# Moving sides of 256 columns in a split-precision decoder layer

## The chip, the cores and the metric

The kernel runs on one core of one Trainium2 chip. The metric is the device time of one execution in microseconds, as the median of the runs; lower is better.

## What is computed

One decoder layer for a single sequence of 256 tokens with 2048 channels, all in float32:

```python
h    = rms_norm(x, norm_gain)
proj = h @ w_in          # [256, 8192]: h_conv | B | C | z_conv | q | k | v | z_attn, 1024 each
y_conv = short_gated_conv(h_conv, B, C, conv_w)            # B * causal 3-tap conv of (C * h_conv)
y_conv = rms_norm(y_conv, conv_out_gain) * silu(z_conv)
q, k   = per-head rms_norm of q and k                      # 8 heads of 128
y_attn = moba_attention(q, k, v)                           # 256 tokens are one block: causal attention
y_attn = rms_norm(y_attn, attn_out_gain) * silu(z_attn)
x      = x + concat([y_conv, y_attn]) @ w_out              # [256, 2048] @ [2048, 2048]
```

## The kernel before

Products of float32 operands are made from split operands: each operand is written as a high part, rounded to the type that TensorE (PE) takes, and a low part, the rest. A product is then three matmuls, high by high, high by low and low by high. ScalarE (ACT) makes the high parts (`wh`, line 462) and VectorE (DVE) the low ones (`wl`, line 463) of every piece of weights, three pieces ahead of the products (`LEAD`). SyncE issues the loads of the pieces.

The products run in three stages, one unit of weights after the other, each unit in pieces:

- Stage A, six units: q, k and v with tokens on the partitions, in chunks of 512 columns. The stationary side is a slice of x (`xs`), 128 channels by 128 tokens, and the weights move, 512 columns at a time. `by_parts` (lines 96 to 101) issues the three matmuls, one line each (99, 100, 101). A unit has 16 slices of channels and two of tokens, so 96 matmuls.
- Stage B, 20 units: the convolution's inputs and the gates with channels on the partitions, in groups of 256 channels. The weights are stationary, 128 channels by 128 columns, and x moves. `by_chan` (lines 466 to 471) moves both parts of x at once: line 470 multiplies `wh` by high and low part side by side, 512 columns, into a whole bank of `acc`, and line 471 adds `wl` by the high part to the first 256 columns. The bank's two halves still have to be added: `added` (lines 333 to 337) copies one half with ACT (line 335) and adds the other with DVE (line 336), and a further DVE product follows (lines 343, 347, 360, 364). A unit has 64 matmuls.
- Stage Y, eight units: the output product. Slices of y (`yh`, `yl`) are stationary, and `w_out` moves, 512 columns at a time, again through `by_parts`. The last unit is treated apart: it keeps three sums in `aux` banks, one of 512 columns for the first 128 tokens and two of 256 for the others, so that little is left to do after the last product.

Attention (`scores`, `attend` and the transposes) uses short matmuls of 128 and 256 columns on PE between the pieces of A and B. Work of the other engines is put into numbered slots (`at`), one for each piece, and issued after that piece's products. `acc` has two buffers of two banks, `aux` four of one.

Of the kernel before, what the change touches and what calls it, by code (L numbers as in the profile page):

```python
# [10 lines left out]
F32 = mybir.dt.float32  # L11
FR = mybir.dt.float32r
BF16 = mybir.dt.bfloat16
AF = mybir.ActivationFunctionType
# [3 lines left out]
P = 128  # L18
# [4 lines left out]
DG = 1024  # L23
CW = 512
HD = 128
NH = DG // HD
# [5 lines left out]
MASKED = -3.0e38  # L32
# w_in's columns: h_conv, b_gate, c_gate, z_conv, q, k, v, z_attn, DG each. q, k and v are computed with tokens on the
# partitions, in chunks of CW columns; the others with channels on the partitions, in groups of GW columns
A_ORDER = [(name, c) for c in range(DG // CW) for name in "qkv"]
B_ORDER = [("a", g) for g in range(NG)] + [(name, g) for g in range(NG) for name in "hcbz"]
FIRST = {name: n * DG for n, name in enumerate("hbczqkva")}
# columns of the parameter array
G_IN, G_Q, G_K, G_C, G_A, C_W = 0, 16, 17, 18, 26, 34
# [9 lines left out]
def hybrid_layer(ctx: ExitStack, tc: tile.TileContext, xT, x, w_a, w_b, w_out, par, out):  # L49
# [12 lines left out]

# [1 line left out]
    prm = cst.tile([P, NPAR], F32, name="prm")  # L64
# [12 lines left out]
    make_identity(nc, ident)  # L77
    # causal mask of the three blocks that a head has: (q0, k0), (q1, k0), (q1, k1)
    msk = cst.tile([P, 3, P], F32, name="msk")
# [4 lines left out]

# [1 line left out]
    todo = {}  # L86
# [4 lines left out]
    def then(slot, f, g, *args):  # L91
        """f now, g with f's result in a later slot"""
        r = f(*args)
        at(slot, g, *args, r)

    def by_parts(acc, stationary, moving, first, last):
        """the product of two split operands, without that of their low parts"""
        (sh, sl), (mh, ml) = stationary, moving
        nc.tensor.matmul(acc, sh, mh, start=first, stop=False)  # L99
        nc.tensor.matmul(acc, sh, ml, start=False, stop=False)  # L100
        nc.tensor.matmul(acc, sl, mh, start=False, stop=last)  # L101

    def rsqrt(dst, ms):
        nc.gpsimd.tensor_tensor(dst, ms, neg_half[:, :ms.shape[-1]], op=OP.pow)  # L104

    # sums of squares over channels, by partition and token: of x, of the attention, of the convolution
    sums = {}

    def add_squares(key, src):
        """src [P, 2, SEQ]"""  # L110
        sq = tp.tile([P, CW], F32, name="sq", bufs=2)
        nc.scalar.activation(sq, src, AF.Square)
        if key not in sums:
            s = sums[key] = cst.tile([P, SEQ], F32, name="sums_" + key)
            nc.vector.tensor_add(s, sq[:, :SEQ], sq[:, SEQ:])
        else:
            for i in range(2):
                nc.vector.tensor_add(sums[key], sums[key], sq[:, i * SEQ:(i + 1) * SEQ])
# [7 lines left out]
    def partition_sums(hi, lo):  # L126
        """on every partition"""
        a = aux()
        nc.tensor.matmul(a[:, :SEQ], ones, hi, start=True, stop=False)
        nc.tensor.matmul(a[:, :SEQ], ones, lo, start=False, stop=True)  # L130
        return a

    def by_token(dst, a):
        """dst [token, NT] from rows a [any, NT * token]"""
        for t in range(NT):
            d = tp.tile([P, P], F32, name="diag", bufs=2)
            nc.vector.tensor_tensor_reduce(out=d, in0=a[:, t * P:(t + 1) * P], in1=ident, scale=1.0, scalar=0.0,
                                           op0=OP.mult, op1=OP.add, accum_out=dst[:, t:t + 1])

    def token_sums(slot, key, f):  # L140
        """f gets the sums over channels [token, NT]"""
        def summed(a):
            ms = tp.tile([P, NT], F32, name="ms_t", bufs=2)
            by_token(ms, a)
            f(ms)

        at(slot, lambda: at(slot + 2, lambda hl=split_rows(sums[key]): at(slot + 3, summed, partition_sums(*hl))))

# [1 line left out]
    xs = cst.tile([P, KT, 2, SEQ], FR, name="xs")  # L150
# [13 lines left out]

    # rx by token on the partitions; rxb, its square rx2b by token along the free axis
    rx = cst.tile([P, NT], F32, name="rx")
# [16 lines left out]

    # y, transposed and split for the products
    yh = cst.tile([P, KT, SEQ], FR, name="yh")
    yl = cst.tile([P, KT, SEQ], FR, name="yl")

# [1 line left out]
    qk_0, v_sb, sq, ssq_h, r_h, qn = {}, {}, {}, {}, {}, {}  # L189
# [65 lines left out]
    def mask(h):  # L255
        # s = -(scale * masked score); its minimum is -max
        s = pr[h] = tp.tile([P, 3 * P], F32, name="s", bufs=3)
        mx[h] = tp.tile([P, NT], F32, name="mx", bufs=2)
        m = msk.rearrange("p b k -> p (b k)")
        for t, sl in parts:  # L260
            nc.vector.tensor_tensor_reduce(out=s[:, sl], in0=sc[h][:, sl], in1=m[:, sl], scale=-scale, scalar=3.0e38,
                                           op0=OP.add, op1=OP.min, accum_out=mx[h][:, t:t + 1])
# [38 lines left out]

# [1 line left out]
    def split_y(y, kt, col):  # L303
# [13 lines left out]
    def c_rms(ms):  # L317
        # the convolution lacks a factor rx: r_c = rx * (rx ** 2 * mean square + EPS) ** -0.5
        nc.vector.tensor_mul(ms, ms, rx)
        nc.vector.tensor_mul(ms, ms, rx)  # L320
        nc.vector.tensor_scalar(ms, ms, 1.0 / DG, EPS, op0=OP.mult, op1=OP.add)
        rsqrt(r_c, ms)
# [3 lines left out]

# [1 line left out]
    h_sb, u_sb, cv, yc, z_sb = {}, {}, {}, {}, {}  # L328

    def by_channel(rows):  # L330
        return rows[:, None, :].to_broadcast([P, GPT, SEQ])

    def added(acc):
        d = t2k((P, GPT, SEQ))
        nc.scalar.activation(d, acc[:, :, SEQ:], AF.Copy)  # L335
        nc.vector.tensor_add(d, acc[:, :, :SEQ], d)  # L336
        return d

    def h_done(g, acc):
        h_sb[g] = added(acc)  # L340

    def h_scaled(g):
        nc.vector.tensor_mul(h_sb[g], h_sb[g], by_channel(rx2b))

    def c_done(g, acc):
        u_sb[g] = added(acc)
        nc.vector.tensor_mul(u_sb[g], u_sb[g], h_sb[g])

# [9 lines left out]
    def b_done(g, acc):  # L358
        yc[g] = added(acc)
        nc.vector.tensor_mul(yc[g], yc[g], cv[g])  # L360

    def z_done(g, acc):
        z_sb[g] = added(acc)
        nc.vector.tensor_mul(z_sb[g], z_sb[g], by_channel(rxb))

# [7 lines left out]

# [1 line left out]
    def v_done(c, t, acc):  # L375
# [28 lines left out]
    def finish_b(name, g, acc, e):  # L404
        if name == "a":
            at(e + 1, z_done, g, acc)
            at(e + 2, z_silu, g)
            at(A_DONE + 2 * g, lambda: z_gate(g, oT[:, g * GPT:(g + 1) * GPT], KT // 2, G_A))
        elif name == "h":
            at(e + 1, h_done, g, acc)  # L410
            at(e + 2, h_scaled, g)
        elif name == "c":
            at(e + 1, c_done, g, acc)
            at(e + 2, conv, g)
        elif name == "b":
            at(e + 1, b_done, g, acc)
            at(e + 2, lambda: add_squares("c", yc[g]))
        else:
            at(e + 1, z_done, g, acc)
            at(e + 2, z_silu, g)  # L420
            at(e + 3, lambda: z_gate(g, yc[g], 0, G_C))

# [1 line left out]
    units = [("A", n, w_a[n], KT) for n in range(len(A_ORDER))] + [("B", n, w_b[n], KT) for n in range(len(B_ORDER))]  # L424
# [41 lines left out]
    def by_chan(acc, k, w, i, first, last):  # L466
        """channels on the partitions: x moves, both its parts at once; the sum of acc's halves is the product"""
        for b in range(GPT):
            wh, wl = (a[:, i, b * P:(b + 1) * P] for a in w)
            nc.tensor.matmul(acc[:, b], wh, xs[:, k].rearrange("p s t -> p (s t)"), start=first, stop=False)  # L470
            nc.tensor.matmul(acc[:, b, :SEQ], wl, xs[:, k, 0], start=False, stop=last)  # L471

# [13 lines left out]

# [1 line left out]
    ends = {}  # L488
# [22 lines left out]
    for j, (kind, n, _, k, last, pk, _) in enumerate(pieces):  # L511
        load(j + LOADS)
        split(j + LEAD)
        if k == 0:
            acc = ps.tile([P, 2, CW], F32, name="acc", bufs=2)
        w = ws.pop(j)
# [13 lines left out]
        else:  # L530
# [8 lines left out]
            else:  # L539
                # the last chunk by three sums, in its last piece one after the other, so that little follows the products  # L540
                order = [(i, t, slice(c * CW // (1 + t), (c + 1) * CW // (1 + t)), acc[t, c][:, :CW // (1 + t)])
# [52 lines left out]
```

## Time and profile before

| | us |
|---|---|
| median of three runs | 475.95 (475.84 to 476.95) |
| span of the profiled execution, first to last instruction | 474.2 |
| TensorE busy | 468.2 |
| VectorE busy | 304.0 |
| ScalarE busy | 242.8 |

The profile shows one execution, and the span is the only total that it gives of it; the runs' median is 1.75 us longer. Matmuls are shown with starts and with modelled ends, and one's end lies behind the next one's start, so their pace is read from the starts. PEld is the weight load that goes ahead of each matmul. A row such as "L470 PE MATMUL acc<-xs,wh" names line, engine, operation, the tile written and the tiles read.

### The profile page before, as it was taken

To read this page: it belongs to the slowest core of one execution; us is meant where nothing else is said; L and a number is where in the kernel's file an instruction comes from. 1 tells how busy PE (TensorE), PEld (TensorE's weight loads), DVE (VectorE), ACT (ScalarE), POOL (GpSimd) and SP (SyncE) were. 2 spreads that over 40 slices of the span, in tenths; PEclk is the share of its full clock that TensorE was granted. 3 is DMA by queue.
4 is the path that set the end of the run, shared out by engine and by line. 5 is a ranking of instruction groups with operands and counts; after the bars stand their busy time and mean duration, and the time that the engine had idled before them with its cause. 6 is when DMAs were issued, how large, how long until landed. Compare 5 with 4: busy or idle time off the path is not lost.

```text
span 474.2 us, 6428 instructions
## 1 busy us (share of the span) xinstructions
PE 468.2 (99%) x2416; PEld 395.6 (83%) x2416; DVE 304.0 (64%) x440; ACT 242.8 (51%) x337; POOL 20.1 (4%) x23
## 2 busy tenths in 40 slices
PE   8999999999999999999999999999999999999996
PEld 5788888888888898888888888888888888888885
DVE  5798766557475657678766675666666675555541
ACT  6875446565544677655555454454545453433320
POOL 1001210002020000000100000000000010000100
PEclk9999999999999999999999999999999999999999
DMA  7977654645464544555565555656555768756611
GB/s 257 349 262 242 218 184 139 217 133 178 136 205 162 195 147 147 177 184 179 189 207 194 188 181 187 203 183 195 194 186 186 219 223 252 241 182 204 203 61 57
DMA packets 27583, 90.63 MB, mean 191 GB/s; under 512 B 3232, under 2 KB 4512, under 8 KB 27552
## 3 DMA queue, kind: packets, MB, share of 16 engines
q1 hardware_dynamic: 27072, 88.65, 57.4%
q0 software_dynamic: 480, 1.57, 1.0%
q8 instruction: 19, 0.31, 0.3%
q14 instruction: 12, 0.10, 0.1%
HBM read 88.11 MB, written 2.10 MB: 190 GB/s over the span
## 4 chain that ended last, share of the span: by engine, by line
PE 98%; DMA 1%; SPq 0%; ACT 0%; DVE 0%; issue 0%; ACTq 0%
PE acc L470 31%; PE acc L471 16%; PE acc L99 15%; PE acc L100 15%; PE acc L101 15%; PE aux L99 1%; PE aux L100 1%; PE aux L101 1%; PE aux L221 1%; DMA prm<-in_par_dram 1%; PE aux L281 1%; PE aux L250 0%; PE aux L297 0%; ACT xs L162 0%; DVE t2k L482 0%; PE aux L130 0%
## 5 line engine op out<-in xcount | busy, mean ns | idle before, releaser
L463 DVE TENSOR_TENSOR wl<-raw,wh 128x1024 fp32r<-128x1024 f32 x156 | 190.3, 1223 | 103.2 <-ACT wh L462 102.4
L462 ACT ACTIVATE wh<-raw 128x1024 fp32r<-128x1024 f32 x156 | 164.6, 1057 | 115.2 <-PE acc L101 62.6
L470 PE MATMUL acc<-xs,wh 128*128 128x512 f32 x640 | 222.6, 392 | 0.0
L471 PE MATMUL acc<-xs,wl 128*128 128x256 f32 x640 | 178.9, 280 | 0.0
L470 PEld LDWEIGHTS acc<-xs,wh 128*128 128x128 f32 x640 | 120.1, 188 | 26.2
L471 PEld LDWEIGHTS acc<-xs,wl 128*128 128x128 f32 x640 | 120.2, 188 | 0.0
L99 PE MATMUL acc<-wh,xs 128*128 128x512 f32 x192 | 77.9, 406 | 0.7 <-ACT xs L162 0.7
L100 PE MATMUL acc<-wl,xs 128*128 128x512 f32 x192 | 76.7, 400 | 0.0
L101 PE MATMUL acc<-wh,xs 128*128 128x512 f32 x192 | 76.5, 399 | 0.0
L99 PEld LDWEIGHTS acc<-wh,xs 128*128 128x128 f32 x192 | 36.6, 191 | 9.6 <-ACT xs L162 1.6
L99 PE MATMUL acc<-wh,yh 128*128 128x512 f32 x112 | 44.5, 397 | 0.0
L101 PE MATMUL acc<-wh,yl 128*128 128x512 f32 x112 | 44.5, 397 | 0.0
L100 PE MATMUL acc<-wl,yh 128*128 128x512 f32 x112 | 44.5, 397 | 0.0
L101 PEld LDWEIGHTS acc<-wh,xs 128*128 128x128 f32 x192 | 36.6, 191 | 9.0
L100 PEld LDWEIGHTS acc<-wl,xs 128*128 128x128 f32 x192 | 36.7, 191 | 8.5 <-DVE wl L463 0.4
L335 ACT ACTIVATE t2k<-acc 128x512 f32<-128x512 f32 x20 | 11.9, 597 | 28.4 <-PE acc L471 28.4
L336 DVE TENSOR_TENSOR t2k<-acc,t2k 128x512 f32<-128x512 f32 x20 | 13.8, 691 | 18.0 <-ACT t2k L335 18.0
L101 PEld LDWEIGHTS acc<-wh,yl 128*128 128x128 f32 x112 | 21.2, 189 | 5.0
L99 PEld LDWEIGHTS acc<-wh,yh 128*128 128x128 f32 x112 | 21.2, 189 | 4.9
L100 PEld LDWEIGHTS acc<-wl,yh 128*128 128x128 f32 x112 | 21.2, 189 | 4.8
L306 ACT ACTIVATE yh<-t2k,prm 128x256 fp32r<-128x256 f32 x16 | 7.3, 502 | 16.8 <-DVE t2k L371 16.8
L104 POOL TENSOR_TENSOR r<-ms,neg_half 128x8 f32<-128x8 f32 x4 | 10.1, 2524 | 80.7 <-DVE ms L208 80.7
(117 smaller groups left out, 289.1 us busy)
## 6 DMA issues: line engine op xcount, KB each, us to landing
raw<-in_w_b_dram SPq DMA_DIRECT2D x80, 512.0 KB, 4.6
raw<-in_w_a_dram SPq DMA_DIRECT2D x44, 512.0 KB, 3.9
raw<-in_w_out_dram SPq DMA_DIRECT2D x32, 512.0 KB, 4.0
raw<-in_w_a_dram SPq DMA_DIRECT2D x8, 256.0 KB, 4.5
t2k<-in_x_dram SPq DMA_DIRECT2D x8, 256.0 KB, 4.8
out_dram<-t2k POOLq DMA_DIRECT2D x6, 256.0 KB, 3.3
t2k<-in_xT_dram SPq DMA_DIRECT2D x8, 128.0 KB, 4.4
t2k<-in_xT_dram SPq DMA_DIRECT2D x4, 256.0 KB, 7.5
```

What stands on the lines that cost most here:

```text
L99: nc.tensor.matmul(acc, sh, mh, start=first, stop=False)
L100: nc.tensor.matmul(acc, sh, ml, start=False, stop=False)
L101: nc.tensor.matmul(acc, sl, mh, start=False, stop=last)
L104: nc.gpsimd.tensor_tensor(dst, ms, neg_half[:, :ms.shape[-1]], op=OP.pow)
L221: nc.tensor.transpose(a[:, i * P:(i + 1) * P], qn[key, t][:, i], ident)
L306: nc.scalar.activation(yh[:, kt + i], src, AF.Copy, scale=g)
L335: nc.scalar.activation(d, acc[:, :, SEQ:], AF.Copy)
L336: nc.vector.tensor_add(d, acc[:, :, :SEQ], d)
L462: nc.scalar.activation(wh, raw, AF.Copy)
L463: nc.vector.tensor_tensor(wl, raw, wh.bitcast(F32), op=OP.subtract)
L470: nc.tensor.matmul(acc[:, b], wh, xs[:, k].rearrange("p s t -> p (s t)"), start=first, stop=False)
L471: nc.tensor.matmul(acc[:, b, :SEQ], wl, xs[:, k, 0], start=False, stop=last)
```

## The change

`by_parts` cuts the moving side into stretches of `NW` = 256 columns: for each of its three parts it issues one matmul per stretch, so that a product of 512 columns is six matmuls of 256 where it was three of 512. `by_chan` calls `by_parts` too: each of the 16 slices and two blocks of channels is three matmuls of 256 columns that all add into the same 256 columns of `acc`, and a group of stage B takes one bank, of which each block of channels has a half. The two halves no longer have to be added, so `added` is gone; `times` multiplies `acc` by the other factor straight away, and `h_scaled`, which was a slot of its own, goes into `h_done`. Comments were taken out, which moves line numbers.

```diff
+NW = 256
     def by_parts(acc, stationary, moving, first, last):
-        """the product of two split operands, without that of their low parts"""
         (sh, sl), (mh, ml) = stationary, moving
-        nc.tensor.matmul(acc, sh, mh, start=first, stop=False)
-        nc.tensor.matmul(acc, sh, ml, start=False, stop=False)
-        nc.tensor.matmul(acc, sl, mh, start=False, stop=last)
+        for n, (s, m) in enumerate(((sh, mh), (sh, ml), (sl, mh))):
+            for i in range(0, CW, NW):
+                if i < acc.shape[-1]:
+                    cols = slice(i, min(i + NW, acc.shape[-1]))
+                    nc.tensor.matmul(acc[:, cols], s, m[:, cols], start=first and n == 0 and i == 0,
+                                     stop=last and n == 2 and cols.stop == acc.shape[-1])
...
-    def added(acc):
+    def times(acc, other):
         d = t2k((P, GPT, SEQ))
-        nc.scalar.activation(d, acc[:, :, SEQ:], AF.Copy)
-        nc.vector.tensor_add(d, acc[:, :, :SEQ], d)
+        nc.vector.tensor_mul(d, acc, other)
         return d
     def h_done(g, acc):
-        h_sb[g] = added(acc)
-
-    def h_scaled(g):
-        nc.vector.tensor_mul(h_sb[g], h_sb[g], by_channel(rx2b))
+        h_sb[g] = times(acc, by_channel(rx2b))
     def c_done(g, acc):
-        u_sb[g] = added(acc)
-        nc.vector.tensor_mul(u_sb[g], u_sb[g], h_sb[g])
+        u_sb[g] = times(acc, h_sb[g])
...
         for b in range(GPT):
-            wh, wl = (a[:, i, b * P:(b + 1) * P] for a in w)
-            nc.tensor.matmul(acc[:, b], wh, xs[:, k].rearrange("p s t -> p (s t)"), start=first, stop=False)
-            nc.tensor.matmul(acc[:, b, :SEQ], wl, xs[:, k, 0], start=False, stop=last)
+            by_parts(acc[:, b], [a[:, i, b * P:(b + 1) * P] for a in w], [xs[:, k, s] for s in range(2)],
+                     first and b == 0, last and b == GPT - 1)
...
-            acc = ps.tile([P, 2, CW], F32, name="acc", bufs=2)
+            acc = (ps.tile([P, GPT, SEQ], F32, name="acc", bufs=2) if kind == "B"
+                   else ps.tile([P, 2, CW], F32, name="acc", bufs=2))
```

`b_done` and `z_done` change as `c_done` does, with `cv[g]` and `by_channel(rxb)`.

On TensorE, where stage A ends and stage B begins, the program before has these rows (a matmul's tile is followed by the size of what it writes):

```order
L99 MATMUL acc<-wh,xs 128x512
L100 MATMUL acc<-wl,xs 128x512
L101 MATMUL acc<-wh,xs 128x512
L470 MATMUL acc<-xs,wh 128x512
L471 MATMUL acc<-xs,wl 128x256
```

At the same place the changed program has these, where "x4" is two matmuls that end one product and two that begin the next:

```order
L105 MATMUL acc<-wh,xs 128x256 x4
L105 MATMUL acc<-wl,xs 128x256 x2
L105 MATMUL acc<-wh,xs 128x256 x2
L105 MATMUL acc<-xs,wh 128x256 x2
L105 MATMUL acc<-xs,wl 128x256
```

Each 512 of stage A has become two 256s in a row, and the 512 and the 256 of stage B three 256s. In the whole program the matmul instructions go from 2400 to 3976.

On VectorE, behind the first products of a group of the convolution (h, then c), the program before has these rows, with the weight splits of line 463 between them:

```order
L336 TENSOR_TENSOR t2k<-acc,t2k 128x512
L463 TENSOR_TENSOR wl<-raw,wh 128x1024
L343 TENSOR_TENSOR t2k<-t2k,rx2b 128x512
L463 TENSOR_TENSOR wl<-raw,wh 128x1024 x3
L336 TENSOR_TENSOR t2k<-acc,t2k 128x512
L347 TENSOR_TENSOR t2k<-t2k 128x512
L463 TENSOR_TENSOR wl<-raw,wh 128x1024
```

The changed program has these there (line 460 is the weight split):

```order
L340 TENSOR_TENSOR t2k<-acc,rx2b 128x512
L460 TENSOR_TENSOR wl<-raw,wh 128x1024 x4
L340 TENSOR_TENSOR t2k<-acc,t2k 128x512
L460 TENSOR_TENSOR wl<-raw,wh 128x1024
L356 SCALAR_TENSOR_TENSOR t2k<-t2k,prm 128x255
```

The addition is gone, and the product that followed it reads `acc` in the addition's place.

## Rows read from the trace of the kernel before

**Rows 1.** The page: span, busy engines, granted clock by slices, chain by engine.
```profile
span 474.2 us, 6428 instructions
...
PE 468.2 (99%) x2416; PEld 395.6 (83%) x2416; DVE 304.0 (64%) x440; ACT 242.8 (51%) x337; POOL 20.1 (4%) x23
...
PEclk9999999999999999999999999999999999999999
...
PE 98%; DMA 1%; SPq 0%; ACT 0%; DVE 0%; issue 0%; ACTq 0%
```

**Rows 2.** Waits of TensorE, whole span: total us, times, longest.
```profile
PE aux L69 <- DVE warm L66: 1.2, 1, 1.2
PE acc L99 <- ACT xs L162: 0.7, 1, 0.7
```

**Rows 3.** Line 470 from 240 to 370 us: count, durations, first and last start.
```profile
L470 PE MATMUL acc<-xs,wh x376: 391/392/392, 239.8 to 369.8; 128*128 128x512 f32 x188
```

**Rows 4.** The same view of line 99 from 384 to 457 us, stage Y.
```profile
L99 PE MATMUL acc<-wh,yh x105: 397/397/398, 383.9 to 456.7; 128*128 128x512 f32 x105
```

**Rows 5.** The same view of line 99 from 127 to 140 us, stage A.
```profile
L99 PE MATMUL acc<-wh,xs x19: 394/394/394, 126.8 to 139.4; 128*128 128x512 f32 x19
```

**Rows 6.** Timeline in stage B: start us, duration us, engine, line, tiles.
```profile
299.36 0.28 PE L471 MATMUL acc<-xs,wl 128*128 128x256 f32 x1
299.36 0.19 PEld L470 LDWEIGHTS acc<-xs,wh 128*128 128x128 f32 x1
299.47 0.39 PE L470 MATMUL acc<-xs,wh 128*128 128x512 f32 x1
...
299.70 0.28 PE L471 MATMUL acc<-xs,wl 128*128 128x256 f32 x1
...
299.82 0.39 PE L470 MATMUL acc<-xs,wh 128*128 128x512 f32 x1
...
300.05 0.28 PE L471 MATMUL acc<-xs,wl 128*128 128x256 f32 x1
...
300.17 0.39 PE L470 MATMUL acc<-xs,wh 128*128 128x512 f32 x1
```

**Rows 7.** Timeline of the last output chunk, the first matmul of each width.
```profile
458.85 0.40 PE L99 MATMUL aux<-wh,yh 128*128 128x512 f32 x1
...
460.25 0.28 PE L99 MATMUL aux<-wh,yh 128*128 128x256 f32 x1
...
461.66 0.40 PE L99 MATMUL aux<-wh,yh 128*128 128x512 f32 x1
...
463.05 0.28 PE L99 MATMUL aux<-wh,yh 128*128 128x256 f32 x1
...
464.41 0.39 PE L99 MATMUL aux<-wh,yh 128*128 128x512 f32 x1
```

**Rows 8.** Timeline of attention work between two pieces of stage A.
```profile
102.25 0.49 PE L281 MATMUL aux<-ident,p 128*128 128x128 f32 x3
102.58 0.39 PE L250 MATMUL aux<-qk,qk 128*128 128x128 f32 x2
...
102.92 0.28 PE L100 MATMUL aux<-yl,yh 128*128 128x256 f32 x1
103.04 0.28 PE L101 MATMUL aux<-yh,yl 128*128 128x256 f32 x1
103.16 0.39 PE L99 MATMUL acc<-wh,xs 128*128 128x512 f32 x1
```

**Rows 9.** Groups of weight loads: count, busy us, mean ns, idle before.
```profile
L130 PEld LDWEIGHTS aux<-row_l,ones 128*128 128x128 f32 x4 | 0.8, 189 | 0.1
L129 PEld LDWEIGHTS aux<-row_h,ones 128*128 128x128 f32 x4 | 0.8, 188 | 0.2
```

**Rows 10.** The page's groups of lines 335 and 336.
```profile
L335 ACT ACTIVATE t2k<-acc 128x512 f32<-128x512 f32 x20 | 11.9, 597 | 28.4 <-PE acc L471 28.4
L336 DVE TENSOR_TENSOR t2k<-acc,t2k 128x512 f32<-128x512 f32 x20 | 13.8, 691 | 18.0 <-ACT t2k L335 18.0
```

More of the change, by code (lines that the diff above doesn't have):

```diff
@@ L358, in b_done @@
     def b_done(g, acc):
-        yc[g] = added(acc)
-        nc.vector.tensor_mul(yc[g], yc[g], cv[g])
+        yc[g] = times(acc, cv[g])
     def z_done(g, acc):
-        z_sb[g] = added(acc)
-        nc.vector.tensor_mul(z_sb[g], z_sb[g], by_channel(rxb))
+        z_sb[g] = times(acc, by_channel(rxb))
     def z_silu(g):
@@ L410, in finish_b @@
             at(e + 1, h_done, g, acc)
-            at(e + 2, h_scaled, g)
         elif name == "c":
```

## The prediction

> **What bounds the kernel now.** I read the page first, for its busy shares and its chain, then the waits of TensorE, then the starts of its matmuls in each stage, and last the end of the program, where matmuls of both widths stand side by side. On the page TensorE (PE) is busy for 99% of the span at a granted clock of 9 tenths or more in every slice, and 98% of the chain that ended last is PE; VectorE (DVE) is busy 64% and ScalarE (ACT) 51% [rows 1]. Once the warm-up is over PE waits for another engine a single time, 0.7 us, for the first slice of x [rows 2]. So the time is the sum of the distances between one matmul's start and the next's, and a change counts only by what it does to those. The durations of matmul rows can't be used for that, since matmuls overlap: one of 512 columns is shown with 392 ns and the next starts after about 230 [rows 3, 6]. I take starts.
>
> In stage B (channels on partitions) 376 matmuls of line 470 start from 239.8 to 369.8 us: 130.0/375 = 346.7 ns for a pair of one 512-column and one 256-column matmul [rows 3]. In stage Y (the output product) 105 matmuls of line 99 start from 383.9 to 456.7: 72.8/104 = 700 ns for three of 512 columns, 233.3 each [rows 4]. Stage A (tokens on partitions) gives the same in a stretch with nothing else in it: 12.6/18 = 700 ns, 233.3 each [rows 5]. Inside the pairs three 256-column matmuls from 299.36 on are followed after 0.11, 0.12 and 0.12 us, about 117 ns on average, which leaves about 230 of the 346.7 for the 512 [rows 6].
>
> **What a 256-column matmul costs among its like.** The change makes every large product of such matmuls, so this one number decides. The nearest rows are the last output chunk, where three accumulators of 512, 256 and 256 columns already run in turns, six matmuls of 512 and twelve of 256 in each turn [rows 7]. In the first turn the six take 460.25 - 458.85 = 1.40 us, 233.3 ns each, just stage Y's price, and the twelve 461.66 - 460.25 = 1.41 us, 117.5 each. In the second the six take 1.39 us, 231.7 each, and the twelve 464.41 - 463.05 = 1.36 us, 113.3 each: the program's last matmuls run faster, for a reason that I can't see in the rows. The attention's short runs stand beside it: two 256-column matmuls take 103.16 - 102.92 = 0.24 us, 120 ns each, and three of 128 columns, half as wide, still take 102.58 - 102.25 = 0.33 us, 110 each [rows 8]. A narrower matmul thus saves next to nothing below 256 columns: each weight load with its matmul has a floor of about 110 ns, and at 117.5 the change puts all products a few ns above it. The rows show this from the other side too: the next load starts when the running matmul starts (299.36 and 299.36), and the matmul that needs it 0.11 to 0.12 us later [rows 6].
>
> The Trainium skill, "TensorE: Matmul & The Clock Gate", section "LDWEIGHTS (loading the stationary operand)", puts a load at columns/1.2 ns, 107 for 128 columns; the 110 ns above agree. Its section "Back-to-back issue gap" gives N/2.4 + 2.5 ns for a matmul, by which each added matmul would cost 2.5 ns, 1576 of them 3.9 us, an estimate that would end at 479.9; but it gives 215.8 ns for 512 columns, where the rows have 233.3, so the rows go ahead.
>
> I take 117.5 ns for the sum: it is the value of the only run of twelve at the price that stages A and Y pay for their 512s, and within a nanosecond that of the 256s in stage B. The bounds are 113.3 and 120.
>
> **The change part by part.** (1) The weights are loaded for every matmul. Consecutive matmuls now share a stationary side, and one might hope for one load; but lines 129 and 130 multiply by the same `ones` in turn today, and each has its load, four and four [rows 9]. So each added matmul adds a load: 576 in A, 336 in Y, 24 in the last chunk and 640 in B, 1576 in all.
>
> (2) A and Y: a 512 becomes two 256s of the same operands: 235.0 for 233.3, +1.7 ns, times 576 + 336 + 6 (the first turn of the last chunk) = 918: +1.6 us. The last chunk's other 18 go from at most 231.7 to 226.6, a tenth of a us, left out. Bounds: 113.3 gives -6.7 each, -6.2 us; 120 gives +6.7, +6.2 us.
>
> (3) B: a 512 and a 256 (xh and xl together, then xh with the low weights) become three 256s: 352.5 for 346.7, +5.8 ns, times 640: +3.7 us. Bounds: 3 x 113.3 = 339.9, -6.8 each, -4.4 us; 3 x 120 = 360, +13.3, +8.5 us. Here the change gives up a 512 that runs at about 230, which is less than in A and Y.
>
> (4) The sum of halves goes: 20 ACT copies of 597 ns, 11.9 us, and 20 DVE additions of 691 ns, 13.8 us [rows 10]. The product that followed each addition reads PSUM now, as the addition did, and so should cost what that cost, 691 ns. All of it lies under PE's chain: DVE and ACT are at 64% and 51%, and PE's rows show no wait for either after the start [rows 1, 2]. I cost it at nothing. The products queue on DVE directly behind PE, without ACT between; behind them wait only weight splits made three pieces ahead.
>
> (5) A B group holds one bank instead of two, and is read once instead of twice; the next but one group needs the buffer a whole group, 32 x 346.7 = 11.1 us, later, so it comes free in good time in both kernels. Three matmuls in a row now add into the same 256 columns; in the last chunk six in a row do, at 117.5 and 113.3, so that has no price of its own. Start and end stay: the first products wait for x, and the last chunk's three sums keep their order.
>
> Sum: +1.6 + 3.7 = +5.3 us. The profiled span of 474.2 becomes 479.5; the median of the runs lies 1.75 us above the span, and with that the time is **481.2 us**, 1.1% slower.
>
> **The rivals.** *Per column.* A 256 costs half of its stage's 512: 116.7 in A and Y (0), and 115 in B, 345 for 346.7, -1.1 us: 474.9. For it: in A, Y and the last chunk's first turn 117.5 is nearly half of 233.3. Against it: B's own 256s stand at about 117, not 115, though nothing else differs there. With 116.7 everywhere B costs +3.4 each, +2.2 us: 478.1. So this case runs from 474.9 to 478.1.
>
> *The fast rate everywhere.* 113.3 in all products, as in the last turns: -6.2 - 4.4 = -10.6 us, 465.3. It would take that the slower rate comes from something that the change removes, such as ACT's and DVE's reads of PSUM. Against: stage Y has none of those copies and additions and still pays 233.3 [rows 4]. The same time comes if equal weights were not loaded twice.
>
> *Pairs of load and matmul don't go out that fast for long.* This is slower, and by more. The longest run of narrow matmuls in the trace is about a dozen, and the sustained mean is 346.7/2 = 173 ns per pair in B; the change asks for 117.5 for 465 us. It decides from 117.5 up: at 120, the attention's price, the sum is +6.2 + 8.5 = +14.7, 490.6 us; every further ns is worth 918 x 2 + 640 x 3 = 3756 ns. Against it: twelve at 113.3 in a row, followed by 512s without a stall. The Trainium skill, same page, section "Wait — 56ns, not 53.3ns?", has a sequencer that spends about 62 ns on each matmul when its decoding is done in firmware; were that so for loads too, a pair would take 124 ns and the time, as an estimate, 505.6; the dozen at 113.3 speak against it.
>
> *The change doesn't do what it says:* the order of the built program shows the matmuls at 256 columns throughout, so I give this nothing.
>
> **How the numbers follow.** The forecast (117 to 118.5 ns, 479 to 485 us) gets 0.52; per column 0.22, of which 0.05 faster, 0.12 same and 0.05 slower by over 0.3%, which is 1.4 us and about what a measurement of this kernel can tell from no change; the fast rate 0.10; the slow pairs 0.16. Together: faster 0.15, same 0.12, slower 0.73. The range leaves out the fast rate and the part of the slow pairs above 120 ns, 0.10 and 0.08: 474 to 491.
>
> **What would show it.** In the changed profile: starts in A, B and Y 117 to 118.5 ns apart (three in B 352, six in A and Y 705); stage B longer by about 4 us, A and Y together by 1.6; about 26 us less of DVE and ACT work, and no trace of that in the end. It would be wrong if the distance is 113 to 115 (time below 477), if loads go missing (fewer load rows than matmuls), if it is 120 or more in long runs with the short ones at 117, or if PE shows waits for DVE or ACT in B.

## The result, and the profile after

The changed kernel takes **484.03 us**, the median of four runs from 483.31 to 484.13, against 476.06 for the kernel before beside it: a ratio of 1.0162, 95% interval 1.0146 to 1.0178. The forecast was 481.2 with a range of 474 to 491 and a chance of 0.73 for slower. Sign and range hold, and the forecast is 2.8 us short; which of its terms was too small is the first question.

The page of the changed kernel, the lines that answer to [rows 1]: span, busy engines, granted clock by slices, chain by engine.

```profile
span 482.4 us, 9549 instructions
...
PE 475.4 (99%) x3992; PEld 472.0 (98%) x3992; DVE 292.1 (61%) x420; ACT 231.9 (48%) x317; POOL 20.2 (4%) x23
...
PEclk9999999999999999999999999999999999999999
...
PE 95%; DMA 2%; SPq 1%; DVE 0%; ACT 0%; issue 0%
```

The waits of TensorE over the whole span (total us, times, longest), as [rows 2]:

```profile
PE aux L70 <- DVE warm L67: 1.2, 1, 1.2
PE acc L105 <- ACT xs L167: 0.8, 1, 0.8
PE acc L105 <- DVE wl L460: 0.8, 1, 0.8
```

TensorE is still the bound and waits for 1.6 us after its warm-up. There are 1576 matmuls more, and as many loads as matmuls, so no load was spared. VectorE and ScalarE each lost 20 instructions and 11 to 12 us of work. The clock is in the top tenth throughout. The time must then lie in the distances between matmuls, stage by stage. The first matmuls of stages A, B and Y and the program's last one stand in the timelines (start us, duration us, engine, line, tiles, count), first of the kernel before:

```profile
5.44 0.80 PE L99 MATMUL acc<-wh,xs 128*128 128x512 f32 x1 [0.66 <-ACT xs L162]
...
152.13 0.40 PE L470 MATMUL acc<-xs,wh 128*128 128x512 f32 x1
...
380.25 0.40 PE L99 MATMUL acc<-wh,yh 128*128 128x512 f32 x1
...
469.76 0.28 PE L101 MATMUL aux<-wh,yl 128*128 128x256 f32 x1
```

and of the changed kernel, where all large products are on line 105:

```profile
5.58 0.50 PE L105 MATMUL acc<-wh,xs 128*128 128x256 f32 x2 [0.80 <-ACT xs L167]
...
155.67 0.40 PE L105 MATMUL acc<-xs,wh 128*128 128x256 f32 x2
...
387.49 0.39 PE L105 MATMUL acc<-wh,yh 128*128 128x256 f32 x2
...
477.97 0.28 PE L105 MATMUL aux<-wh,yl 128*128 128x256 f32 x1
```

| stage | before, us | after, us | difference | forecast |
|---|---|---|---|---|
| A, from the first product to B's first | 146.69 | 150.09 | +3.4 | +1.0 (576 x 1.7 ns) |
| B | 228.12 | 231.82 | +3.7 | +3.7 |
| Y with the last chunk | 89.51 | 90.48 | +1.0 | +0.6 |

B is as forecast, Y nearly, A is not. The paces tell why. In stage A the low weights' pairs of 256 columns come once in six matmuls; the first and the last of 25 such rows:

```profile
130.57 0.40 PE L105 MATMUL acc<-wl,xs 128*128 128x256 f32 x2
...
147.85 0.40 PE L105 MATMUL acc<-wl,xs 128*128 128x256 f32 x2
```

17.28 us/24 = 720 ns for six, **120.0 each**, where three of 512 took 700 [rows 5]. In stage Y, the first and the last of 17 rows:

```profile
419.90 0.40 PE L105 MATMUL acc<-wh,yl 128*128 128x256 f32 x2
...
431.21 0.40 PE L105 MATMUL acc<-wh,yl 128*128 128x256 f32 x2
```

11.31/16 = 706.9 for six, **117.8 each**. In B, grouped by tiles from 240 to 370 us (count, durations, first and last start), to be read beside [rows 3]:

```profile
L105 PE MATMUL acc<-xs,wl x370: 277/280/282, 239.9 to 369.8; 128*128 128x256 f32 x185
```

129.9/369 = 352.0 for three, 117.3 each. So 256 columns cost 120.0 where x is loaded and 117.8 where y is, with the same weights moving; the width alone doesn't set the price.

### The profile page after: what moved, and what is told of

Same layout as the page of the kernel before. It is cut to its first block, busy times and chain, and to the rows that moved or that the text cites. A ratio compares the mean times of both kernels' runs of the same rounds, so it can differ in the third digit from the quotient of the medians.

```text
span 482.4 us, 9549 instructions
## 1 busy us (share of the span) xinstructions
PE 475.4 (99%) x3992; PEld 472.0 (98%) x3992; DVE 292.1 (61%) x420; ACT 231.9 (48%) x317; POOL 20.2 (4%) x23
## 4 chain that ended last, share of the span: by engine, by line
PE 95%; DMA 2%; SPq 1%; DVE 0%; ACT 0%; issue 0%
PE acc L105 89%; PE aux L105 4%; DMA raw<-in_w_a_dram 1%; DMA t2k<-in_xT_dram 1%; PE aux L226 1%; PE aux L286 1%; SPq L436 0%; PE aux L255 0%; PE aux L302 0%; SPq L161 0%; DVE wl L460 0%; ACT wh L459 0%; DVE t2k L478 0%; PE aux L135 0%; PE aux L134 0%
## 5 line engine op out<-in xcount | busy, mean ns | idle before, releaser
L105 PE MATMUL acc<-xs,wh 128*128 128x256 f32 x1280 | 226.3, 280 | 0.0
L105 PEld LDWEIGHTS acc<-xs,wh 128*128 128x128 f32 x1280 | 195.7, 188 | 0.0
L105 PE MATMUL acc<-wh,xs 128*128 128x256 f32 x768 | 127.6, 284 | 0.9 <-ACT xs L167 0.8
L105 PEld LDWEIGHTS acc<-wh,xs 128*128 128x128 f32 x768 | 106.6, 188 | 2.2 <-ACT xs L167 1.7
L105 PE MATMUL acc<-wl,xs 128*128 128x256 f32 x384 | 77.2, 282 | 0.8 <-DVE wl L460 0.8
L105 PEld LDWEIGHTS acc<-wl,xs 128*128 128x128 f32 x384 | 59.5, 189 | 1.0 <-DVE wl L460 1.0
L105 PE MATMUL acc<-wl,yh 128*128 128x256 f32 x224 | 44.6, 279 | 0.0
L105 PE MATMUL acc<-wh,yl 128*128 128x256 f32 x224 | 44.4, 279 | 0.0
L105 PE MATMUL acc<-wh,yh 128*128 128x256 f32 x224 | 44.4, 279 | 0.0
L105 PEld LDWEIGHTS acc<-wh,yl 128*128 128x128 f32 x224 | 34.2, 188 | 0.0
```

The source lines that it names most:

```text
L105: nc.tensor.matmul(acc[:, cols], s, m[:, cols], start=first and n == 0 and i == 0, stop=last and n == 2 and cols.stop == acc.shape[-1])
```

## The experiments

**1. The price of a matmul by itself.** Ahead of the last chunk, blocks of 48 matmuls were added to the kernel before, one width and one loaded tile each; x, y, a copy of x, and loads of only 64 columns.

```diff
+        for s, mv, c, f, l in seq(y2, w, 256):
+            nc.tensor.matmul(m[:, c], s, mv, start=f, stop=l)
+        for s, mv, c, f, l in seq(x2, w, 256):
+            nc.tensor.matmul(m[:, c], s, mv, start=f, stop=l)
+        for s, mv, c, f, l in seq(y2, w, 256, 64):
+            nc.tensor.matmul(m[:64, c], s, mv, start=f, stop=l)
...
```

> The kernel before, with eleven runs of 48 further matmuls into a spare bank just ahead of the last output chunk, on operands of the products; their output goes nowhere. Read is the distance from one start to the next. Theory 1, the weight load sets a floor: a matmul can't start sooner than about 110 to 118 ns after the one ahead, because its 128 columns of weights have to be loaded while that one runs. Then 256 columns take 117 to 118 with y as weights, 128 columns about 110, and with weights of 64 columns both fall: 256 to half of what 512 takes (at most 116.7, likely 113), 128 to 60 to 80; 512 gains little from short weights (228 to 233). Theory 2, each matmul has a fixed price of 2 to 5 ns beside its columns, whatever its weights: 128 columns take 58 to 65 ns with either weights, 256 columns 117 to 118 with either. On stage A's own price (120 ns in the changed kernel, 117.8 in Y): if the layout of x is the cause (high and low part side by side in one tile), x as weights gives 120 here too and copies of x in two tiles 118; if it is something that runs beside stage A, all three give 118. Stage B's three of 256 give 117.3 as in the changed kernel. The run takes about 85 us longer.

The first matmul of each block in the timeline of this kernel; what stands behind `128*` is the number of columns loaded:

```profile
458.02 0.40 PE L508 MATMUL aux<-wh,yh 128*128 128x512 f32 x1
...
469.22 0.28 PE L510 MATMUL aux<-wh,yh 128*128 128x256 f32 x1
...
474.88 0.39 PE L512 MATMUL aux<-wh,xs 128*128 128x512 f32 x1
...
486.07 0.40 PE L514 MATMUL aux<-wh,xs 128*128 128x256 f32 x2
...
491.83 0.40 PE L516 MATMUL aux<-wh,t2k 128*128 128x256 f32 x2
...
497.59 0.40 PE L518 MATMUL aux<-wh,yh 128*64 128x256 f32 x2
...
503.19 0.44 PE L520 MATMUL aux<-wh,yh 128*128 128x128 f32 x3
...
508.50 0.41 PE L522 MATMUL aux<-wh,yh 128*64 128x128 f32 x4
511.38 0.39 PE L524 MATMUL aux<-wh,yh 128*128 128x384 f32 x1
...
519.75 0.39 PE L526 MATMUL aux<-wh,yh 128*64 128x512 f32 x1
...
530.71 0.40 PE L529 MATMUL aux<-xs,wh 128*128 128x256 f32 x2
```

Differences of neighbours over 48: y 233.3 at 512 columns and 117.9 at 256, x 233.1 and 120.0, the copy of x 120.0. At 128 columns the mean is 110.6 with loads of 128 columns (a first step of 58 and then 111.7) and 60.0 with loads of 64 (and an output of half the partitions): there the load does set it. At 256, however, short loads save 1.2 ns (117.9 to 116.7), so the load's floor is not what makes 256 columns dear. At 512 they go with 5 ns less (228.3 for 233.3). Stage B's three of 256 were expected at 117.3 as in the changed kernel and took 118.7 each here (the 48 start from 530.71 to 536.29 us): blocks and kernel don't agree for B.

The Trainium skill, "TensorE: Matmul & The Clock Gate", section "Step-by-step: what each phase is for", says that "Loading the next tile's weights doesn't steal SBUF read bandwidth from the running matmul." These 5 ns would speak against it if they came from the shorter loads. That isn't shown: y takes 228.9 with whole loads too, in the same steps of 226 to 232 ns, in the second set of blocks of experiment 4, so the short loads may only have met y's other price. No run here settles the page's statement.

**2. Each half of the change alone.** In one kernel only stage B has 256 columns, in the other only A, Y and the last chunk.

```diff
 # the changed kernel, with 256 columns in B alone
-NW = 256
+NW = 512
```

```diff
 # the kernel before, with 256 columns in A and Y
-        nc.tensor.matmul(acc, sh, mh, start=first, stop=False)
-        nc.tensor.matmul(acc, sh, ml, start=False, stop=False)
-        nc.tensor.matmul(acc, sl, mh, start=False, stop=last)
+        for n, (s, m) in enumerate(((sh, mh), (sh, ml), (sl, mh))):
+            for i in range(0, CW, NW):
...
```

> The changed kernel with stretches of 512 columns: A and Y as before, B with three matmuls of 256 and no sum of halves. Theory (price per start): B's 228.1 us become 231.8, all else stays, +3.7 us: 479.8, ratio 1.008. Rival (the runs are longer for another reason, such as more instructions to fetch in the whole program): less than +2 us here, since two thirds of the added matmuls are not in it.

> The kernel before with by_parts cut at 256 columns: A and Y as changed, B as before, sum of halves kept. Theory: A +3.4 and Y with the last chunk +1.0 us, 480.5, ratio 1.009, and with the run of B alone the two add up to the whole change (+8.0). On A's price: 120 ns again, so the cause isn't the changed stage B. Rival: A at 117.5 here, +1.0, 478.0.

Both came out at 479.86 us: B alone 1.0079 of the kernel before (1.0054 to 1.0105), A and Y alone 1.0091 (1.0068 to 1.0114). With 475.88 for the kernel before, each half costs 4.0 us, and the two add up to the 8.0 of the whole: they don't act on each other.

**3. The sum of halves.** The kernel before with its own matmuls, but with the products of VectorE reading one half of the bank instead of copy, addition and product; the other half is left out of the sum.

```diff
-        nc.scalar.activation(d, acc[:, :, SEQ:], AF.Copy)
-        nc.vector.tensor_add(d, acc[:, :, :SEQ], d)
+        nc.vector.tensor_mul(d, acc[:, :, :SEQ], other)
```

> The kernel before with its matmuls, but without the 20 copies and 20 additions: the product that follows reads the first half of the bank alone, so that the part of the sum from x's low part is left out. Theory: the 25.7 us of ScalarE and VectorE work lie under the matmuls and are worth nothing: 476.0 within 0.3%, B's pair 346.7 ns. Rival: those reads of PSUM slow the matmuls beside them, and without them B runs at 340 to 345 ns a pair, 472 to 475.

475.71 us, ratio 1.0006 (0.9990 to 1.0022): some 11 us less work on each of two engines is worth nothing, and stage B takes 228.1 us in the profiled execution, as before. Where the sums went, the changed kernel has one product with PSUM, priced as the addition in [rows 10] was; the largest of its groups (count, busy us, mean ns, idle before and what ended it):

```profile
L340 DVE TENSOR_TENSOR t2k<-acc,t2k 128x512 f32<-128x512 f32 x8 | 5.5, 691 | 4.1 <-PE acc L105 4.1
```

**4. Does a change of width make the matmuls faster?** In [rows 7] the price falls behind the first turn of 512s and 256s. If the alternation did that, A and Y in the same order (six of 512, then twice six of 256) would gain.

```diff
-            for i in range(pk):
-                for t in range(NT):
+            for t, c in ((0, slice(0, CW)), (1, slice(0, SEQ)), (1, slice(SEQ, CW))):
+                for i in range(pk):
```

> The kernel before, with stages A and Y in the order of its last output chunk: per piece six matmuls of 512 columns for the first 128 tokens, then six and six of 256 for the others. B unchanged. Theory 3, the pace depends on the run of widths: a long uniform run falls into a slow step (233.3 for 512, 117.8 for 256) and a change of width gets it out (about 229 and 113.3, as the last chunk's later turns show, here and in the run of B alone): a turn of 18 takes 6 x 229 + 12 x 113.3 = 2734 ns for 2800, A and Y lose 66 ns for each of some 76 turns, 5.0 us: 471, ratio 0.989. Rival, the last turns are fast because the program ends there: 512 at 233.3 and 256 at 117.8 throughout, 2813 ns a turn, +1 us: 477, ratio 1.002.

477.74 us, ratio 1.0047 (1.0032 to 1.0062): the gain of 5 us did not come. Matmuls of 256 columns took 120 ns with x and 117.8 with y, and 512 columns stayed at 233.4 with x; only the 512s of Y ran at 229, as the theory has it.

A second set of blocks, 96 matmuls each, then put the uniform and the mixed orders side by side.

```diff
+        for s, mv, c, f, l in whole(y2, w, 512):
...
+        for s, mv, c, f, l in mixed(y2, w):
...
+        for s, mv, c, f, l in whole(y2, w, 512):
...
```

> The kernel before with ten runs of 96 further matmuls into a spare bank ahead of the last output chunk. Theory 3: uniform 512 with y 233.3, then six 512 and twelve 256 in turns 229 and 113.3, uniform 512 again 233.3 or, if the fast step holds once found, 229; three 512 and six 256 in turns fast as well; the same with x as weights fast. If the widths don't matter: 233.3 and 117.8 in all. On the 120 ns with x: if the distance between the addresses of high and low weights decides (16 KB for y, 1 or 2 KB for x), x with slices 16 KB apart gives 117.8 and y with slices 2 KB apart 120; otherwise 120 and 117.8. For stage B: 512, 256 in turns 346.7 a pair, two 512 then two 256 perhaps less (fast step 342), three of 256 352 to 356.

The first and the third block are one and the same code (grouped by line, first and last of 32 starts, 31 x 3 = 93 steps apart):

```profile
L522 PE MATMUL aux<-wh,yh x32: 397/397/398, 459.0 to 480.7; 128*128 128x512 f32 x32
...
L526 PE MATMUL aux<-wh,yh x32: 388/388/388, 496.5 to 517.8; 128*128 128x512 f32 x32
```

21.7/93 = 233.3 and 21.3/93 = 229.0. So products with y have two prices, 233.3 or 228.9 at 512 columns and 117.8 or 113.3 at 256. The price changes in the mixed block between the two (the first matmul of each run of one width):

```profile
482.77 0.28 PE L524 MATMUL aux<-wh,yh 128*128 128x256 f32 x1
...
484.19 0.40 PE L524 MATMUL aux<-wh,yh 128*128 128x512 f32 x1
...
485.57 0.28 PE L524 MATMUL aux<-wh,yh 128*128 128x256 f32 x1
...
486.93 0.39 PE L524 MATMUL aux<-wh,yh 128*128 128x512 f32 x1
```

The twelve 256s take 1.42 us in the first turn, 118 each, and 1.36 in the second, 113.3 each; the six 512s between them take 230. In this block as in [rows 7] the lower price sets in with the first 512s behind a run of 256s, and here the uniform block that follows keeps it. For y that is what theory 3 expected of these blocks; in Y of the mixed kernel the 512s had the lower price and the 256s didn't, and why is open. Products with x stayed near 120 at 256 columns in both orders, also with its slices read 16 KB apart. In stage B's orders, 512 and 256 in turns took 346.7 a pair, two and two 351.6 where the theory had 342.

**5. Values or place?** x, y and zeros were copied one after the other into the same pair of tiles, and each copy was loaded for 96 matmuls.

```diff
+        xa = copied(x2)
+        for s, mv, c, f, l in whole(xa, w, 256):
...
+        ya = copied(y2)
...
+        za = copied(y2, 0.0)
...
```

> The kernel before with eight runs of 96 further matmuls into a spare bank ahead of the last output chunk: as weights y itself, then, in one and the same pair of tiles, copies of x, of y and of zeros (256 columns), of x and of y (512 columns), then x itself and y itself again (256 columns). The question is why x as weights has 120 ns where y has 113 to 118, in three layouts so far. If places in SBUF decide, the copies all have one price, 120 as the copies of x in other tiles had. If the values decide, the copy of x has 120, the copy of y 113.3 to 117.8, and zeros no more than y; for 512 columns 233.5 with x and 228.9 or 233.3 with y.

Copies of x (line 511), of y (514) and zeros (517) at 256 columns, x itself (525) and y itself (527):

```profile
L511 PE MATMUL aux<-wh,sq x64: 279/283/283, 470.4 to 481.8; 128*128 128x256 f32 x64
L514 PE MATMUL aux<-wh,sq x64: 278/283/386, 482.7 to 494.2; 128*128 128x256 f32 x64
L517 PE MATMUL aux<-wh,sq x64: 278/283/386, 495.0 to 506.5; 128*128 128x256 f32 x64
L525 PE MATMUL aux<-wh,xs x64: 276/279/285, 552.0 to 563.4; 128*128 128x256 f32 x64
L527 PE MATMUL aux<-wh,yh x32: 276/276/276, 563.5 to 573.8; 128*128 128x256 f32 x32
```

95 steps in 11.4 to 11.5 us, 120 to 121 ns for each of the copies: y and even zeros at x's price, once they lie in another tile, and the same pair of tiles gave 226.7 at 512 columns, in the steady part of its blocks. y itself takes 10.3 us for some 91 steps, 113. **What is loaded doesn't matter, where it lies does.**

**6. A sweep over places.** The loaded columns were taken from 20 places in x's tile, 0 to 896 bytes further, for 48 matmuls each; then the same with x as the moving side, as in B.

```diff
+        for e in SHIFTS:
+            for s, mv, c, f, l in times_48(as_y(flat, e, w, 512)):
+                nc.tensor.matmul(m[:, c], s, mv, start=f, stop=l)
...
```

> The kernel before with 60 runs of 48 further matmuls into a spare bank ahead of the last output chunk, on the same moving weights of w_out, with the stationary side read from x's tile at 20 distances from its start, 0 to 896 bytes; first 512 columns as in Y, then 256 as in Y, then 512 and 256 in turns as in B, with the 512 and 256 moved out of x's tile from the same places. If the place of the weights against that of the moving side decides the price, as the copies in one pair of tiles showed, the price of 512 goes between 226.7 and 233.5 with the distance and comes back at a period; 256 between 113.3 and 120 not at the same places; 96 bytes (the copies' place) gives 226.7 and 120, 0 bytes gives 233.5 and 120, 32 bytes (y's place) 228.9 or 233.3 and 113.3 or 117.8. If it is which part of the memory the tile lies in, and not its distance, all are 233.5 and 120.

First and last rows of equal kind in four of the blocks: 512 columns at 0 and at 96 bytes (15 and 14 steps of three), 256 columns at 32 and at 96 (7 and 6 steps of six):

```profile
458.49 0.40 PE L507 MATMUL aux<-wl,xs 128*128 128x512 f32 x1
...
468.99 0.39 PE L507 MATMUL aux<-wl,xs 128*128 128x512 f32 x1
...
525.00 0.39 PE L507 MATMUL aux<-wl,xs 128*128 128x512 f32 x1
...
534.52 0.39 PE L507 MATMUL aux<-wl,xs 128*128 128x512 f32 x1
...
692.63 0.28 PE L510 MATMUL aux<-wl,xs 128*128 128x256 f32 x1
...
697.39 0.28 PE L510 MATMUL aux<-wl,xs 128*128 128x256 f32 x1
...
715.03 0.40 PE L510 MATMUL aux<-wl,xs 128*128 128x256 f32 x2
...
719.35 0.40 PE L510 MATMUL aux<-wl,xs 128*128 128x256 f32 x2
```

| bytes further | 0 | 16 | 32 | 64 | 96 | 112 | 128 | 160 | 192 |
|---|---|---|---|---|---|---|---|---|---|
| 512 columns, ns | 233.4 | 229.9 | 228.9 | 233.3 | 226.7 | 226.7 | 233.2 | 233.4 | 234.2 |
| 256 columns, ns | 120.0 | 118.1 | 113.3 | 116.7 | 120.0 | 118.3 | 118.4 | 113.3 | 120.0 |
| B's pair, ns | 346.7 | 350 | 353.3 | 346.7 | 346.7 | 346.7 | 346.7 | 353.4 | 350 |

(Prices are those of the steady part of a block; the first few steps of each block differ. From 192 bytes on 512 columns stay between 232.5 and 234.4, and 256 between 116.8 and 120.1.) The two widths have their good places apart: at 96 bytes 512 columns are at their best and 256 at their worst, at 160 256 are at their best and 512 take 233.4. These are the prices seen before, 233.3 and 226.7, 120.0 and 113.3, and here the place alone was changed. The tile of y lies where the sweep's 32 lies, modulo 1024 bytes, and y's lower prices are the sweep's there.

**7. The whole kernels at two other places.** Both kernels were run with the tiles of x and y begun 32 or 96 bytes into a KB, by allocating small tiles earlier; no instruction is changed. Where the tiles begin in their partition, modulo 1024 bytes:

```
                  xs    yh, yl   wh, wl
as they were      960   992      32
place 32          32    32       32     (the sweep's 96)
place 96          96    96       32     (the sweep's 160)
```

```diff
+    rx, r_a, r_c = (cst.tile([P, NT], F32, name=n) for n in ("rx", "r_a", "r_c"))
+    cst.tile([P, 16], F32, name="gap")
     xs = cst.tile([P, KT, 2, SEQ], FR, name="xs")
...
+    cst.tile([P, 240], F32, name="gap2")
```

(place 96; place 32 has the first line alone, and the later lines that allocated these tiles go in both.)

> The kernel before with three small tiles (rx, r_a, r_c) allocated ahead of x's tile, so that x and y begin 96 and 64 bytes further on and all else stays: modulo 1024 bytes x, y and the split weights now begin at the same place, the 96 bytes of the sweep. Theory (distance of the two sides' places): 512 columns 226.7 for 233.3 in A and Y, 576 + 336 times 6.6 ns, -6.0 us; B's pair 346.7 as before (116.4 and 230.3 in the sweep): 470.0, ratio 0.987. Rival (the sweep's operands were too few, the products run over many slices and five weight buffers): 233.3 still, 476.

> The changed kernel with the same three tiles moved. Theory: at this distance 256 columns have 120.0: A unchanged (720 for six), Y 720 for 706.7, +1.5 us; B's three of 256 not in the sweep, 350 to 358: about 485.5 and 482 to 490. The change would then cost 15 us at this place where it costs 8 at the old one. Rival: 484.

> The kernel before with the tiles moved and a gap of 64 bytes ahead of x: x and y begin 64 bytes behind the weights' place modulo 1024, the 160 bytes of the sweep. Theory: 512 columns 233.4, A and Y as before; B's pair 119.8 + 233.6 = 353.4, +4.3 us: 480.3, ratio 1.009. Rival (places don't carry over to the products): 476.

> The changed kernel at the same place. Theory: 256 columns have 113.3 here: six in A 680 for 720, -7.7 us, in Y 680 for 706.7, -3.0 us; B's three of 256 between 350 and 358 (-1 to +4 us): 473 to 477, so that at this place the change is faster than the kernel before by 3 to 7 us, where at the old place it is slower by 8. Rival: 484, slower than before at the same place.

| place | kernel before, us | with the change, us | the change |
|---|---|---|---|
| as it was | 476.06 | 484.03 | +1.7% |
| 32 | 474.79 | 490.53 | +3.3% |
| 96 | 477.72 | 475.12 | -0.5% |

The percentages are of the two medians beside them; the ratio with the interval in the section on the result was 1.0162. The same edit, with the same instructions, costs 15.7 us at one place and gains 2.6 at another. At place 32 the kernel before, in Y and in B (grouped by line):

```profile
L99 PE MATMUL acc<-wh,yh x108: 389/389/397, 384.0 to 456.7; 128*128 128x512 f32 x108
...
L468 PE MATMUL acc<-xs,wh x369: 395/398/404, 239.9 to 370.0; 128*128 128x512 f32 x185
```

72.7/107 = 679.4 ns for three, 226.5 each, as the sweep has it. B's pair takes 130.1/368 = 353.5, though, where the sweep gave 346.7; so the kernel gained 1.3 us and not the 6 expected: by the starts of their stages A and Y gained 5.4 us and B lost 3.8. At place 96 B's pair misses the sweep as well (129.8/372 = 348.9 where 353.4 was expected), and the kernel before comes at 477.72 for 480.3:

```profile
L470 PE MATMUL acc<-xs,wh x373: 392/392/397, 239.9 to 369.7; 128*128 128x512 f32 x187
```

With the change, at place 32, stage A (24 rows, 23 steps of six) and B:

```profile
131.11 0.40 PE L105 MATMUL acc<-wl,xs 128*128 128x256 f32 x2
...
147.67 0.40 PE L105 MATMUL acc<-wl,xs 128*128 128x256 f32 x2
```

```profile
L105 PE MATMUL acc<-xs,wl x362: 280/283/288, 239.9 to 369.9; 128*128 128x256 f32 x181
```

16.56/23 = 720, 120.0 each, and 130.0/361 = 360.1 for B's three, 120.0 each: every product at the dearest price, and the time above the 482 to 490 expected. With the change at place 96, stages A and Y (36 and 176 matmuls, two in each turn of six, so 103 and 523 steps) and B:

```profile
L105 PE MATMUL acc<-wl,xs x36: 276/276/276, 126.9 to 138.6; 128*128 128x256 f32 x36
...
L105 PE MATMUL acc<-wh,yh x176: 276/276/276, 390.2 to 449.5; 128*128 128x256 f32 x176
```

```profile
L105 PE MATMUL acc<-xs,wl x369: 279/279/279, 239.9 to 370.0; 128*128 128x256 f32 x185
```

11.7/103 = 113.6 and 59.3/523 = 113.4, the sweep's price, and 130.1/368 = 353.5 for three in B; 475.12 lies in the 473 to 477 expected, a gain of 2.6 where 3 to 7 was. So at both places the sweep's prices hold in A and Y, where the loaded side was moved, and those for B's pair do not. This kernel runs in 0.9979 of the kernel before (0.9962 to 0.9997), and the kernel before at place 32 in 0.9974 (0.9960 to 0.9988): the two best of the study, too close together to call either the better.

## Why the prediction came out as it did

**The bound and the method** held. TensorE stayed at 99%, its waits after the warm-up come to 1.6 us, and the three stages' differences add up to 8.1 of the 8.2 us by which its last matmul starts later; the other 0.1 is at the start.

**Stage B** is the term that was right: +3.7 forecast, +3.7 measured in the stage, +4.0 with B alone. Three of 256 columns were put at 352.5 ns and took 352.0. That is in part luck: the price was read where y is loaded and seen again in B's pairs, and at the other places the pairs don't foretell it. At place 32 the 256 of a pair is followed after 117.0 ns and each of the three takes 120.0; at place 96 it is 118.9 and 117.8.

**Stage A** is the mis-sized term: 117.5 ns for a matmul, +1.0 us, against 120.0 and +3.4. The step that failed is the choice of the row. The 117.5 came from the last chunk, where y is loaded, and was carried over to x because at 512 columns both pay 233.3. At 256 they differ. The nearest row that had 120, the attention's [rows 8], was kept as a bound and not as a price. With 120.0 the same step gives 576 x 6.7 = 3.8. What makes x dearer than y is where it lies: in the sweep 256 columns take 120.0 at x's own place and 113.3 at y's.

**Stage Y** came out 0.4 us dearer than forecast: 117.8 rather than 117.5, and the last chunk keeps that price to its end, where [rows 7] had 113.3 from its second turn on. The prediction left their price as it was and costed the difference at nothing. The kernel before becomes faster there because y goes over to its lower price at the first 512s behind a run of 256s, as in the mixed block; the changed kernel has no 512s, and its chunk never does. Why a change of width does this is not shown.

**The sum of halves** at nothing, one **load for every matmul**, and the product's 691 ns held, each by a row above.

**The floor of 110 ns** is real, 111.7 at 128 columns and 60.0 for half the load, but what was read from it isn't borne out. The prediction put 117.5 a few ns above the floor and read the 0.11 to 0.12 us between B's starts as the wait for the load; with half the load a matmul of 256 columns still costs 116.7, and with the whole load 113.3 to 120.0, so the length of the load doesn't set that price.

**The rivals.** *Per column* fell at all three places: at place 32 a 256 takes 120.0 and a 512 of A or Y 226.7, at place 96 113.3 and 233.3. *Slow pairs* named stage A's true price, 120, for a cause that isn't the one: sustained runs go at 113.4 over a whole stage at place 96. Its 490.6 us for 120 ns throughout is what place 32 gave: 490.53. *The fast rate everywhere* was given 0.10 and rejected because Y paid 233.3 without copies; the run without the sums kept B at 228.1 us, but the place brings it, in A and Y. The prediction thus had the right bounds and no idea of what chooses between them.

**What stays open.** Why the place matters. Whether the reads of the next load and of the running matmul get in each other's way isn't shown: what short loads saved lies within y's two prices. Only the loaded side (A, Y) or the moving side (B) was moved, the weights' tiles stayed, so whether the distance between the two decides or each place by itself is not told apart. Why a change of width takes y to its lower price is open, and why the 256s of the mixed kernel didn't follow. So is stage B, whose prices in the kernels at places 32 and 96 are not those of the blocks. A kernel with each stage at its own best place wasn't tried: x is loaded in A and moves in B, from one tile.

## What to carry to other kernels

Where TensorE is the bound and has no waits, take prices from starts, and only from rows that load the same tile and move the same one: a price from another tile of the same shape was 2% off here. Before an edit of widths is judged, run both versions with the tiles begun elsewhere, here 64 to 160 bytes further on; the edit's effect went from +3.3% to -0.5% by that alone. Work taken off engines that TensorE doesn't wait for was worth nothing here, 11 us on each of two.

## What the runs showed of the hardware

- Start to start, a matmul of 256 columns with its load of 128 takes 113.3 to 120.0 ns and one of 512 takes 226.7 to 234.4, by the place of the loaded tile (experiments 5 to 7, x, y and copies loaded); the values don't matter, zeros included.
- Behind the first step of their blocks, 384 columns took 173.3 ns, 128 columns 111.7, and 128 columns with loads of 64 took 60.0. The Trainium skill, "TensorE: Matmul & The Clock Gate", section "LDWEIGHTS (loading the stationary operand)", gives columns/1.2 ns for a load, so 107 and 53: the rows lie 5 and 7 ns above. Whether the load or the matmul holds the 60.0 no run shows.
- The same code on the same operands can run at one of two prices for a hundred matmuls, 233.3 or 228.9 (the two uniform blocks of experiment 4), with the granted clock in the top tenth of every slice and no wait in the blocks; the lower one set in at the first 512s behind a run of 256.
